# Scatter products of an expert: one two-bank PSUM tile and 1024-column adds

## The chip, the cores and the metric

The kernel runs on one core of a Trainium2 chip. The metric is the device time of one launch in microseconds (us). The time before is 1429.59 us, the median of three runs (1428.54 to 1430.69).

## The reference

One decoder block for 256 tokens of width 2048, all in float32: a mixing half (attention heads and a gated recurrence) and then a mixture of experts. Each token takes one of four groups of experts and two of the four experts in it. What matters here is the second half:

```python
for gi in range(N_GROUPS):
    sl = slice(gi * EXPERTS_PER_GROUP, (gi + 1) * EXPERTS_PER_GROUP)
    a = jnp.einsum('nd,edf->nef', hf, w_gate[sl])
    u = jnp.einsum('nd,edf->nef', hf, w_up[sl])
    hid = jax.nn.silu(a) * u * combine[:, sl, None]
    out = out + jnp.einsum('nef,efd->nd', hid, w_down[sl])
```

There are 16 experts of 2048 x 1024 (gate, up) and 1024 x 2048 (down), 24 MB each. `combine` is zero for the experts that a token does not take.

## The kernel before

The mixing half fills the first third of the time and ends at about 480 us. The change is in the expert loop behind it, from L845 on.

**One expert.** Its tokens, at most 64 (`CAP`), are collected by `gather(e)`, L763: eight matmuls with a 0/1 matrix, four into each of two PSUM tiles of 512 columns, one copy by ScalarE out of each tile (L777), then transposes (L783) and VectorE products (L786) into `xg`. The stages `ga` and `up` (L823) and `pd` (L880) each read eight pieces of weights of 1 MB. Two matmuls for the two halves of PSUM's partitions use 64 columns of the array each. ScalarE copies `pd` into `osb` (L883): 128 partitions, of which rows 0 to 63 hold the even blocks of 512 output columns and rows 64 to 127 the odd ones, for the same 64 tokens.

**Scatter.** `scatter(e)`, L805, brings these rows back to the tokens. For each half j of the columns, each half n of the tokens and each partition half z there is one matmul with 64 rows (L811) into a PSUM tile `psc` of 512 columns, and one add by VectorE (L813) into the accumulator `acc`: eight matmuls and eight adds. The scatter of an expert is written in the loop of the next one. That of expert 0 runs after `up` of expert 1, that of expert 1 between the pieces of `up` of expert 2, and those of experts 2 to 14 between the pieces of `ga` of the next expert. The last expert is different: its weights come in four blocks of columns (L893), each followed by four smaller scatter matmuls (L901) and adds (L906).

**PSUM.** `pscr()` gives tiles of one bank from two tags of two buffers each: `psc` for the products of gather and scatter, `pt` for transposes. With `ga`, `up` (one bank each) and `pd` (two) all eight banks are taken.

**Order.** The instructions of an engine are put in their order when the kernel is built, by a planner with costs of its own: where the next instruction by program order is not ready in its reckoning, it takes the next one that is. A tile of a tag is given out in program order, when the one before in its buffer has been read for the last time. So scatter and gather matmuls stand between the pieces of weights. On the chip each engine then works strictly in that order.

**Weights.** SyncE issues a load of 1 MB for each piece, over 19 slots in SBUF that are used in turn. A load waits until its slot has been read, and for the load eight before it.

Of the kernel before, what the change touches and what calls it, by code (L numbers as in the profile page):

```python
# [9 lines left out]
F32 = mybir.dt.float32  # L10
# [4 lines left out]
AF = mybir.ActivationFunctionType  # L15
ALU = mybir.AluOpType
# [3 lines left out]
P = 128  # L20
# [17 lines left out]
def hybrid_block_kernel(  # L38
# [8 lines left out]
    mm = nc.tensor.matmul  # L47
    V = nc.vector
    S = nc.scalar
# [8 lines left out]
    def area(s, shape, dtype=F32, name="ar"):  # L58

        return arena.tile(shape, dtype, name=name, tag=f"a{s}")  # L60
# [161 lines left out]
    def slot_of(idx):  # L222
        return first[idx] if idx < NSLOT else cycle[(idx - NSLOT) % len(cycle)]
# [158 lines left out]
    for col, w in half1:  # L382
        j, c = w // P, col // P
# [233 lines left out]
    x2 = X  # L617
# [133 lines left out]
    pq = tc.alloc_tile_pool(name="pq", bufs=1, space=PSUM)  # L751
# [5 lines left out]
    def piece(e, kind, i):  # L757
        return loaded.pop((e * 3 + kind) * 8 + i)

    def pscr(tag="psc"):  # L760
        return pq.tile([P, 512], F32, name=tag, tag=tag, bufs=2)

    def gather(e):  # L763

        pg = mp.tile([P, NT, CAP], F32, name="pg")
        for n in range(NT):
            V.tensor_scalar(pg[:, n], slot[:, :CAP], rk[:, n, e:e + 1], r2[:, n:n + 1],  # L767
                            ALU.is_equal, ALU.mult)
        xn = mp.tile([P, 2, 512], F32, name="xn")
        for j in range(2):  # L770
            ps = pscr()
            for n in range(NT):
                for z in range(2):
                    b = 2 * j + z
                    mm(ps[64 * z:64 * z + 64], pg[:, n], x2[:, n, b * 512:(b + 1) * 512],  # L775
                       start=n == 0, stop=n == 1)
            S.activation(xn[:, j], ps, AF.Copy)  # L777
        xg = mp.tile([P, NC, CAP], F32, name="xg")
        for j in range(2):
            pt = pscr("pt").rearrange("p (q z s) -> p q z s", q=4, z=2)  # L780
            xq = xn[:, j].rearrange("s (p q) -> s q p", q=4)
            for q in range(4):
                nc.tensor.transpose(pt[:, q].rearrange("p z s -> p (z s)"), xq[:, q], ident)  # L783
            for z in range(2):
                c0 = (2 * j + z) * 4
                V.tensor_tensor(xg[:, c0:c0 + 4], pt[:, :, z],  # L786
                                gfe[:, c0:c0 + 4].unsqueeze(2).to_broadcast([P, 4, CAP]),
                                ALU.mult)
        return xg

    def scatter_matrix(e):
        pcm = mp.tile([P, NT, P], F32, name="pcm")
        for n in range(NT):
            V.tensor_scalar(pcm[:, n], slot, rk[:, n, e:e + 1], comb[:, e // 4, n, e % 4:e % 4 + 1],
                            ALU.is_equal, ALU.mult)
        pt = pscr("pt").rearrange("p (n s) -> p n s", n=4)
        for n in range(NT):
            nc.tensor.transpose(pt[:, n], pcm[:, n], ident)
        pT = mp.tile([P, NT, P], F32, name="pT")
        V.tensor_copy(pT, pt[:, 0:2])  # L800
        return pT

    acc = [None, None]

    def scatter(e, pT, osb):  # L805
        for j in range(2):
            for n in range(NT):
                for z in range(2):
                    lo = 64 * z
                    ps = pscr()  # L810
                    mm(ps, pT[lo:lo + 64, n], osb[lo:lo + 64, j], start=True, stop=True)  # L811
                    bs = slice((2 * j + z) * 512, (2 * j + z + 1) * 512)
                    V.tensor_tensor(acc[n][:, bs], x2[:, n, bs] if e == 0 else acc[n][:, bs],  # L813
                                    ps, ALU.add)

    def stream(ps, xg, e, kind):
        for i in range(8):
# [11 lines left out]
    def final_gain():  # L829
        sl = [slot_of((NE - 1) * 24 + i) for i in (5, 6, 7)]  # L830
        gf = area(sl[0], [P, D], name="gf")
        y = [area(sl[1 + n], [P, D], name=f"y{n}") for n in range(NT)]
        for q in range(4):
            ps = pscr("pt").rearrange("p (c f) -> p c f", c=4)
            for c in range(4):
                mm(ps[:, c], ident[0:16, 4 * q + c:4 * q + c + 1].to_broadcast([16, P]), frow,
                   start=True, stop=True)
            S.activation(gf[:, q * 512:(q + 1) * 512], ps.rearrange("p c f -> p (c f)"), AF.Copy)
        return sl, gf, y
# [5 lines left out]
    for e in range(NE):  # L845
        ga = pq.tile([P, 512], F32, name="ga")
        up = pq.tile([P, 512], F32, name="up")
        stream(ga, xg, e, 0)
        if e == NE - 1:
            sl, gf, y = final_gain()  # L850
        stream(up, xg, e, 1)
        if e == 0:
            for n in range(NT):
                acc[n] = area(alias[n], [P, D], name=f"acc{n}")
            work = area(alias[2], [P, 2048], name="work")
            osb = work[:, 0:1024].rearrange("p (j f) -> p j f", j=2)
            hid = work[:, 1024:1536]
            hT = work[:, 1536:2048].rearrange("p (j s) -> p j s", j=4)
        silu = S.activation(hid, ga, AF.Silu).ins
        if e == NE - 1:  # L860
            with tc.issue_after(silu):
                S.activation(rf[:, 0:1], rf[:, 0:1], AF.Sqrt)
        V.tensor_tensor(hid, hid, up, ALU.mult)  # L863
        if pend is not None:
            scatter(*pend)
        pT = scatter_matrix(e)
        if e + 1 < NE:
            xg = gather(e + 1)
        pt = pscr("pt").rearrange("p (j s) -> p j s", j=4)
        for j in range(4):  # L870
            nc.tensor.transpose(pt[:, j], hid[:, j * P:(j + 1) * P], ident)
        V.tensor_copy(hT, pt)  # L872
        pd = pq.tile([P, 2, 512], F32, name="pd")
        if e < NE - 1:
            for i in range(8):
                wt = piece(e, 2, i)
                z, j = i // 4, i % 4
                for blk in range(4):
                    lo = 64 * (blk % 2)
                    mm(pd[lo:lo + 64, blk // 2], hT[:, j, z * 64:z * 64 + 64],  # L880
                       wt[:, blk * 512:(blk + 1) * 512], start=i == 0, stop=i == 7)
                advance()
            S.activation(osb, pd, AF.Copy)  # L883
            pend = (e, pT, osb)
# [3 lines left out]
    for b in range(4):  # L888
        for hf in range(2):
            wt = piece(NE - 1, 2, 2 * b + hf).rearrange("p (c f) -> p c f", c=4)  # L890
            for j in range(4):
                for z in range(2):
                    mm(pd[64 * z:64 * z + 64, b % 2, 0:256], hT[:, j, hf * 64:hf * 64 + 64],  # L893
                       wt[:, j, z * 256:(z + 1) * 256], start=hf == 0 and j == 0,
                       stop=hf == 1 and j == 3)
        S.activation(osl[:, b], pd[:, b % 2, 0:256], AF.Copy)
        bs = slice(b * 512, (b + 1) * 512)
        pz = [pscr() for z in range(2)]
        for n in range(NT):
            for z in range(2):  # L900
                mm(pz[z][:, n * 256:(n + 1) * 256], pT[64 * z:64 * z + 64, n],  # L901
                   osl[64 * z:64 * z + 64, b], start=True, stop=True)
        for n in range(NT):
            for z in range(2):
                zs = slice(b * 512 + z * 256, b * 512 + z * 256 + 256)
                V.tensor_tensor(acc[n][:, zs], acc[n][:, zs], pz[z][:, n * 256:(n + 1) * 256],  # L906
                                ALU.add)
        for n in range(NT):
            jk = cst.tile([P, 512], BF16, name="jk", tag="jk", bufs=1)
            S.activation(jk, acc[n][:, bs], AF.Square, accum_out=fs[:, n, b:b + 1])  # L910
            (V if b == 3 else nc.gpsimd).tensor_tensor(y[n][:, bs], acc[n][:, bs], gf[:, bs],
                                                       ALU.mult)
# [14 lines left out]
    with tc.If(nover > CAP):  # L927
        with tc.tile_pool(name="ovp", bufs=1, space=PSUM) as ovp:
# [3 lines left out]
            for n in range(NT):  # L932
                xs = area(free.pop(), [P, D], name="xs")
                V.tensor_scalar(xs, x2[:, n], r2[:, n:n + 1], None, ALU.mult)
                for c in range(NC):
                    pt = ovp.tile([P, P], F32, name="pt", tag="pt", bufs=2)
# [7 lines left out]
            with tc.For_i(0, NE, 1) as e:  # L944
# [12 lines left out]
                for fb in range(2):  # L957
                    for kind, src in ((0, w_gate), (1, w_up)):
                        ps = ovp.tile([P, NT, 512], F32, name="ps", tag="ps", bufs=2)
# [10 lines left out]
                    for j in range(4):  # L970
                        for n in range(NT):
                            pt = ovp.tile([P, P], F32, name="pt", tag="pt", bufs=2)
                            nc.tensor.transpose(pt, hd[:, n, j * P:(j + 1) * P], ident)
                            V.tensor_copy(hTo[:, 4 * fb + j, n * P:(n + 1) * P], pt)
                for b in range(4):
                    ps = ovp.tile([P, NT, 512], F32, name="ps", tag="ps", bufs=2)
                    for c in range(0, 8, 4):
                        wt = rows4(w_down, c, b * 512)
                        for k in range(4):
                            for n in range(NT):  # L980
                                mm(ps[:, n], hTo[:, c + k, n * P:(n + 1) * P], wt[:, k],
                                   start=c + k == 0, stop=c + k == 7)
                    for n in range(NT):
                        bs = slice(b * 512, (b + 1) * 512)
# [38 lines left out]
```

## Time and profile before

| | |
|---|---|
| median of 3 runs | 1429.59 us |
| the profiled execution | 1428.93 us |
| its span, first to last instruction | 1427.2 us |
| busy share: PE, VectorE (DVE), ScalarE (ACT), GpSimd | 95%, 31%, 19%, 1% |
| mean granted clock of TensorE | 0.996 |
| moved by DMA | 483.79 MB |

Times in the profile are counted from the first instruction. PE is TensorE's matmuls, PEld its weight loads, SPq the queue of SyncE. A float32 matmul stands as two records, so "x2" on L811, L775, L823 or L880 is one matmul of the program, and a piece of weights is "x8". In the rows, "x4" after a time counts instructions that were merged because nothing else of that engine came between, and the brackets hold the idle time before them and what ended it.

### The profile page before, as it was taken

Reading aid. Unit: us, or ns where it says so; the run is one execution under the profiler, and the core shown is the slowest. Engines: PE = TensorE matmul, PEld = TensorE weight load, DVE = VectorE, ACT = ScalarE, POOL = GpSimd, SP = SyncE. Lnnn points to the kernel's source line nnn. Section 1 sums busy time; section 2 is a strip of 40 time slices with the busy share of each in tenths; the row PEclk is TensorE's granted clock in tenths of the full one; section 3 lists DMA queues with packets and bytes.
Section 4 is the critical chain, followed back from the end, with each engine's and each line's share of the span. In section 5 each row is a group of like instructions: output and inputs, shape, how many; then the busy total and the mean of one; then the engine's idle time right before and its main releaser. Section 6 shows DMA issues by size and latency. Waiting matters only on the chain.

```text
span 1427.2 us, 16870 instructions
## 1 busy us (share of the span) xinstructions
PE 1357.8 (95%) x7073; PEld 737.6 (52%) x7073; DVE 439.8 (31%) x714; ACT 273.7 (19%) x408; POOL 18.0 (1%) x47
## 2 busy tenths in 40 slices
PE   7999999999999999999999999999999999999995
PEld 6999898898887633433332332323323333233333
DVE  4554557557555410221112111111111111211012
ACT  5453543533533300000000000000000000000012
POOL 2000000000000000000000000000000000000002
PEclk9999999999999999999999999999999999999998
DMA  6566553555697699999999999999999999999995
GB/s 229 186 210 169 162 176 120 176 177 178 219 343 292 228 384 418 422 421 422 420 421 422 421 422 421 422 420 421 421 422 422 420 422 421 421 421 421 421 413 214
DMA packets 111648, 483.79 MB, mean 339 GB/s; under 512 B 19728, under 2 KB 21968, under 8 KB 63440
## 3 DMA queue, kind: packets, MB, share of 16 engines
q1 hardware_dynamic: 110912, 482.62, 85.5%
q8 instruction: 57, 0.93, 0.3%
q14 instruction: 23, 0.19, 0.0%
q10 hardware_dynamic: 656, 0.04, 0.0%
HBM read 480.54 MB, written 2.10 MB: 338 GB/s over the span
## 4 chain that ended last, share of the span: by engine, by line
PE 94%; DVE 2%; ACT 1%; issue 1%; DMA 0%; SPq 0%; DVEq 0%; ACTq 0%
PE ga L823 16%; PE up L823 16%; PE pd L880 15%; PE psc L811 7%; PE pp L310 5%; PE pp L312 5%; PE pp L311 5%; PE pp L293 4%; PE pp L295 4%; PE pp L296 4%; PE psc L775 4%; PE pt L783 1%; PE pw L414 1%; PE pd L893 1%; ACT work L883 1%
## 5 line engine op out<-in xcount | busy, mean ns | idle before, releaser
L823 PE MATMUL ga<-wt,xg 128*64 128x512 f32 x1024 | 272.3, 601 | 0.0
L823 PE MATMUL up<-wt,xg 128*64 128x512 f32 x1024 | 228.0, 595 | 0.0
L263 DVE TENSOR_TENSOR whl<-raw,whl 128x1024 fp32r<-128x1024 f32 x144 | 175.6, 1224 | 136.1 <-ACT whl L262 135.9
L880 PE MATMUL pd<-wt,work 128*64 128x512 f32 x960 | 210.0, 594 | 4.0 <-DVE work L872 4.0
L262 ACT ACTIVATE whl<-raw 128x1024 fp32r<-128x1024 f32 x144 | 152.0, 1058 | 233.4 <-PE pp L312 121.5
L813 DVE TENSOR_TENSOR acc<-acc,psc 128x512 f32<-128x512 f32 x112 | 74.4, 686 | 378.3 <-PE psc L811 378.3
L823 PEld LDWEIGHTS ga<-wt,xg 128*64 128x64 f32 x1024 | 78.8, 136 | 149.0 <-issue 139.8
L293 PE MATMUL pp<-hTh,whl 128*128 128x256 f32 x512 | 147.7, 288 | 3.1 <-ACT hTh L328 3.1
L295 PE MATMUL pp<-hTl,whl 128*128 128x256 f32 x512 | 146.5, 286 | 0.9 <-DVE hTl L329 0.9
L296 PE MATMUL pp<-hTh,whl 128*128 128x256 f32 x512 | 146.2, 286 | 0.0
L823 PEld LDWEIGHTS up<-wt,xg 128*64 128x64 f32 x1024 | 72.5, 137 | 135.0 <-issue 127.7
L880 PEld LDWEIGHTS pd<-wt,work 128*64 128x64 f32 x960 | 69.2, 137 | 134.3 <-issue 123.9
L811 PE MATMUL psc<-work,pT 64*128 64x512 f32 x240 | 99.7, 642 | 16.5 <-ACT work L883 15.4
L293 PEld LDWEIGHTS pp<-hTh,whl 128*128 128x128 f32 x512 | 99.4, 194 | 4.2 <-ACT hTh L328 4.0
L295 PEld LDWEIGHTS pp<-hTl,whl 128*128 128x128 f32 x512 | 99.4, 194 | 1.5 <-DVE hTl L329 1.4
L296 PEld LDWEIGHTS pp<-hTh,whl 128*128 128x128 f32 x512 | 99.4, 194 | 0.0
L883 ACT ACTIVATE work<-pd 128x1024 f32<-128x1024 f32 x15 | 15.3, 1023 | 429.0 <-PE pd L880 429.0
L775 PE MATMUL psc<-X,pg 128*64 128x512 f32 x256 | 94.8, 596 | 0.7 <-DVE pg L767 0.7
L863 DVE TENSOR_TENSOR work<-work,up 128x512 f32<-128x512 f32 x16 | 11.0, 687 | 244.4 <-PE up L823 244.4
L777 ACT ACTIVATE xn<-psc 128x512 f32<-128x512 f32 x32 | 19.0, 595 | 308.2 <-PE psc L775 308.2
L310 PE MATMUL pp<-whl,hTh 128*128 128x512 f32 x192 | 77.6, 404 | 0.0
L312 PE MATMUL pp<-whl,hTl 128*128 128x512 f32 x192 | 75.4, 393 | 0.0
(240 smaller groups left out, 1054.7 us busy)
## 6 DMA issues: line engine op xcount, KB each, us to landing
wt<-in_w_gate_dram SPq DMA_DIRECT2D x128, 1024.0 KB, 19.8
wt<-in_w_up_dram SPq DMA_DIRECT2D x128, 1024.0 KB, 19.8
wt<-in_w_down_dram SPq DMA_DIRECT2D x126, 1024.0 KB, 19.8
raw<-in_w_in_dram SPq DMA_DIRECT2D x55, 1024.0 KB, 5.2
raw<-in_w_out_dram SPq DMA_DIRECT2D x16, 1024.0 KB, 5.3
X<-in_x_dram SPq DMA_DIRECT2D x4, 512.0 KB, 7.1
wt<-in_w_down_dram SPq DMA_DIRECT2D x4, 512.0 KB, 11.4
out_dram<-y SPq DMA_DIRECT2D x4, 512.0 KB, 4.3
```

Source lines behind the costliest of these rows:

```text
L262: S.activation(t[:, 0], raw[:, k * hf:k * hf + k], AF.Copy)
L263: V.tensor_tensor(t[:, 1], raw[:, k * hf:k * hf + k], t[:, 0].bitcast(F32), ALU.subtract)
L293: mm(o, hi[:, k, cs], ah, start=st and j % 2 == 0, stop=False, skip_group_check=True)
L295: mm(o, hi[:, k, cs], al, start=False, stop=False, skip_group_check=True)
L296: mm(o, lo[:, k, cs], ah, start=False, stop=sp, skip_group_check=True)
L310: mm(pp[:, n], ah, hi[:, k], start=c == c0, stop=False)
L312: mm(pp[:, n], al, hi[:, k], start=False, stop=c == c1 - 1)
L775: mm(ps[64 * z:64 * z + 64], pg[:, n], x2[:, n, b * 512:(b + 1) * 512], start=n == 0, stop=n == 1)
L811: mm(ps, pT[lo:lo + 64, n], osb[lo:lo + 64, j], start=True, stop=True)
L813: V.tensor_tensor(acc[n][:, bs], x2[:, n, bs] if e == 0 else acc[n][:, bs], ps, ALU.add)
L823: mm(ps[64 * z:64 * z + 64], xg[:, c], wt[:, o:o + 512], start=c == 0, stop=c == NC - 1)
L880: mm(pd[lo:lo + 64, blk // 2], hT[:, j, z * 64:z * 64 + 64], wt[:, blk * 512:(blk + 1) * 512], start=i == 0, stop=i == 7)
```

## The change

`psc` becomes a tile of two banks with one buffer, where there were two buffers of one bank. In `gather` both halves j go into one tile. In `scatter` the products of z = 0 and z = 1 go into the two banks of one tile, and one add over 1024 columns takes the place of two over 512. The last expert's blocks take their two product tiles as the two banks of one. The bytes of PSUM are the same, and so are the matmuls.

```diff
-    def pscr(tag="psc"):
-        return pq.tile([P, 512], F32, name=tag, tag=tag, bufs=2)
+    def pscr():
+        return pq.tile([P, 512], F32, name="pt", tag="pt", bufs=2)
+
+    def ptwo():
+
+        return pq.tile([P, 2, 512], F32, name="psc", tag="psc", bufs=1)
...
         xn = mp.tile([P, 2, 512], F32, name="xn")
+        ps = ptwo()
         for j in range(2):
-            ps = pscr()
...
-                    mm(ps[64 * z:64 * z + 64], pg[:, n], x2[:, n, b * 512:(b + 1) * 512],
+                    mm(ps[64 * z:64 * z + 64, j], pg[:, n], x2[:, n, b * 512:(b + 1) * 512],
                        start=n == 0, stop=n == 1)
-            S.activation(xn[:, j], ps, AF.Copy)
+            S.activation(xn[:, j], ps[:, j], AF.Copy)
...
     def scatter(e, pT, osb):
         for j in range(2):
             for n in range(NT):
+                ps = ptwo()
                 for z in range(2):
                     lo = 64 * z
-                    ps = pscr()
-                    mm(ps, pT[lo:lo + 64, n], osb[lo:lo + 64, j], start=True, stop=True)
-                    bs = slice((2 * j + z) * 512, (2 * j + z + 1) * 512)
-                    V.tensor_tensor(acc[n][:, bs], x2[:, n, bs] if e == 0 else acc[n][:, bs],
-                                    ps, ALU.add)
+                    mm(ps[:, z], pT[lo:lo + 64, n], osb[lo:lo + 64, j], start=True, stop=True)
+                bs = slice(j * 1024, (j + 1) * 1024)
+                V.tensor_tensor(acc[n][:, bs], x2[:, n, bs] if e == 0 else acc[n][:, bs],
+                                ps.rearrange("p z f -> p (z f)"), ALU.add)
...
-        pz = [pscr() for z in range(2)]
+        p2 = ptwo()
+        pz = [p2[:, z] for z in range(2)]
```

## Rows read from the trace of the kernel before

**Rows 1.** A stretch of the run, PE to POOL: busy us by engine, granted clock, DMA share, GB/s.
```profile
540.00:1380.00 840.00, 798.36 (x3476) 273.62 (x3473) 137.11 (x273) 43.48 (x64) 0.00 (x0) 1.00 1.01 421
```
**Rows 2.** Waits of PE from 540 us: total us, times, longest; the two largest.
```profile
PE pt L871 <- DVE xg L786: 19.7, 14, 1.6
PE psc L811 <- ACT work L883: 15.4, 13, 1.2
```
**Rows 3.** The chain that ended last: start us, us, work; two experts' down stages.
```profile
1044.99 13.98 PE pd L880 x64
...
1103.07 13.98 PE pd L880 x64
```
**Rows 4.** Timeline of SyncE's queue: start us, us; loads of eight pieces each.
```profile
1070.63 17.74 SPq L236 DMA_DIRECT2D wt<-in_w_down_dram  x8
1090.51 17.73 SPq L233 DMA_DIRECT2D wt<-in_w_gate_dram  x8
```
**Rows 5.** Timeline of PE at the end: the last block of the last expert.
```profile
1408.49 3.67 PE L893 MATMUL pd<-wt,work 128*64 128x256 f32 x32
```
**Rows 6.** Line L242, last ten loads: durations ns, first and last start; landing.
```profile
L242 SPq DMA_DIRECT2D wt<-in_w_down_dram x10: 368/1242/9264, 1370.3 to 1397.7; - x10
...
DMA to landing us min/median/max: 11.3/14.0/20.7
```
**Rows 7.** Timeline of PE: scatter of expert 9 between the pieces of `ga`.
```profile
1060.12 1.12 PE L811 MATMUL psc<-work,pT 64*128 64x512 f32 x2 [1.18 <-ACT work L883]
1061.18 1.94 PE L823 MATMUL ga<-wt,xg 128*64 128x512 f32 x8
1063.04 1.12 PE L811 MATMUL psc<-work,pT 64*128 64x512 f32 x2
...
1065.96 1.13 PE L811 MATMUL psc<-work,pT 64*128 64x512 f32 x4
...
1074.74 1.12 PE L811 MATMUL psc<-work,pT 64*128 64x512 f32 x2
1075.79 0.64 PE L775 MATMUL psc<-X,pg 128*64 128x512 f32 x1
```
**Rows 8.** Groups of VectorE by shape, whole run: busy us, mean ns, idle before.
```profile
L813 DVE TENSOR_TENSOR acc<-acc,psc 128x512 f32<-128x512 f32 x112 | 74.4, 686 | 378.3 <-PE psc L811 378.3
...
L567 DVE TENSOR_TENSOR kq<-pp,rd 128x1024 f32<-128x1024 f32 x2 | 2.5, 1226 | 0.6 <-PE pp L296 0.6
```
**Rows 9.** Timeline of all engines: the scatter of expert 0.
```profile
570.07 1.13 PE L811 MATMUL psc<-work,pT 64*128 64x512 f32 x4
...
571.23 1.28 DVE L813 TENSOR_TENSOR acc<-X,psc 128x512 f32<-128x512 f32 x2 [0.29 <-PE psc L811]
571.97 1.72 PE L811 MATMUL psc<-work,pT 64*128 64x512 f32 x4 [0.77 <-DVE acc L813]
...
577.80 3.65 PE L775 MATMUL psc<-X,pg 128*64 128x512 f32 x16
```
**Rows 10.** Timeline of PE: the scatter of expert 1 and the gather behind it.
```profile
617.26 1.13 PE L811 MATMUL psc<-work,pT 64*128 64x512 f32 x4
...
620.18 1.12 PE L811 MATMUL psc<-work,pT 64*128 64x512 f32 x2
...
628.96 1.12 PE L811 MATMUL psc<-work,pT 64*128 64x512 f32 x2
...
631.78 3.60 PE L775 MATMUL psc<-X,pg 128*64 128x512 f32 x16
```
**Rows 11.** Timeline of all engines: the first gather, and a matmul of the second.
```profile
491.87 0.60 ACT L777 ACTIVATE xn<-psc 128x512 f32<-128x512 f32 x1 [1.07 <-PE psc L775]
...
492.44 1.07 PE L775 MATMUL psc<-X,pg 128*64 128x512 f32 x2
...
493.45 0.75 PE L783 MATMUL pt<-ident,xn 128*128 128x128 f32 x4
```
**Rows 12.** Line L233, loads issued from 585 to 592 us.
```profile
DMA to landing us min/median/max: 10.9/11.7/12.5
```

More of the change, by code (lines that the diff above doesn't have):

```diff
@@ L774, in gather @@
                     b = 2 * j + z
-                    mm(ps[64 * z:64 * z + 64], pg[:, n], x2[:, n, b * 512:(b + 1) * 512],
+                    mm(ps[64 * z:64 * z + 64, j], pg[:, n], x2[:, n, b * 512:(b + 1) * 512],
                        start=n == 0, stop=n == 1)
-            S.activation(xn[:, j], ps, AF.Copy)
+            S.activation(xn[:, j], ps[:, j], AF.Copy)
         xg = mp.tile([P, NC, CAP], F32, name="xg")
         for j in range(2):
-            pt = pscr("pt").rearrange("p (q z s) -> p q z s", q=4, z=2)
+            pt = pscr().rearrange("p (q z s) -> p q z s", q=4, z=2)
             xq = xn[:, j].rearrange("s (p q) -> s q p", q=4)
@@ L795, in scatter_matrix @@
                             ALU.is_equal, ALU.mult)
-        pt = pscr("pt").rearrange("p (n s) -> p n s", n=4)
+        pt = pscr().rearrange("p (n s) -> p n s", n=4)
         for n in range(NT):
@@ L833, in final_gain @@
         for q in range(4):
-            ps = pscr("pt").rearrange("p (c f) -> p c f", c=4)
+            ps = pscr().rearrange("p (c f) -> p c f", c=4)
             for c in range(4):
@@ L868, in hybrid_block_kernel @@
             xg = gather(e + 1)
-        pt = pscr("pt").rearrange("p (j s) -> p j s", j=4)
+        pt = pscr().rearrange("p (j s) -> p j s", j=4)
         for j in range(4):
```

## The prediction

> **What bounds the kernel now.** I read the stretches first, then PE's waits, the chain, SyncE's queue and the end of the run. From 540 to 1380 us two things are full at once: the DMA engines (share 1.01, 421 GB/s) and PE (798.36 of 840 us, granted clock 1.00); VectorE is busy 137 us of 840 [rows 1]. Which one sets the end? PE's two largest waits there are for other engines, 19.7 and 15.4 us over the experts, and no wait for a load is of that size [rows 2]. So PE is the chain. It needs 1103.07 - 1044.99 = 58.08 us for an expert [rows 3]. The loads take 1090.51 - 1070.63 = 19.88 us for eight pieces, 59.64 us for the 24 of an expert [rows 4]. PE thus eats up its lead in loaded weights by 1.6 us with each expert, and at the end little of it is left: the last load is issued at 1397.7 and takes at least 11.3 us, so it lands at 1409.0 or later [rows 6], and the half block that reads it starts at 1408.49 + 3.67 / 2 = 1410.3 [rows 5]. That is the key to the case: time added to PE's chain comes out at the end in full, while of time taken from it about 1.3 us can be cashed before the loads are the bound. With the last load's two halves used apart it is 3.67 / 4 = 0.9 us more, 2.2 at most.
>
> **The change part by part.** *Adds.* Eight of 0.686 us become four over 1024 columns. A 1024-column product with an input of two PSUM banks stands in the trace at 1.226 us [rows 8]; bounds are 1.22 and 2 x 0.686 = 1.37. An expert's adds fall from 5.49 to 4.90 us, on an engine that waits 378 us for these very products [rows 8]: nothing on the path.
>
> *Matmuls in the steady experts.* The number of matmuls is the same. What counts is how they stand: one alone occupies PE for 1.12 us and two neighbours (z = 0 and 1) together for 1.13 us [rows 7], so the halves run side by side when adjacent. In the 13 `ga` stages from expert 3 on, the eight stand before the pieces as 1, 1, 2, 2, 1, 1 (the two groups left out in [rows 7] are a pair and a single): six groups, and a group costs PE 1061.18 - 1060.12 = 1.06 us. Four groups would be the least. Will the new tile draw the halves together? I think not by itself. The single at the start had two free buffers and still stood alone, so it was not the buffer that parted the halves but the length of the gap that the planner saw before the next piece. The new tile changes nothing in the lengths of gaps. The places 1, 1, 2, 2, 1, 1 happen to fall on whole tiles (first, second; pair; pair; seventh, eighth), so that no tile has to wait within a gap. I take 0 per expert; one group more or fewer would be +-1.06 us, 13.8 us over 13 experts.
>
> *The wait that one buffer adds.* The first matmul of a tile now waits for the last one's add. By [rows 9] an add starts 571.23 - 570.07 = 1.16 us after its pair; it lasts 1.23, and PE resumes 0.05 us after an add's end (571.23 + 0.69 = 571.92, 571.97): 2.44 us from pair to pair. Queued behind the waiting matmul on PE is everything, the pieces of weights first. Between two tiles in a `ga` stage stands a piece, 1063.04 - 1061.18 = 1.86 us, and the next pair comes 1.06 + 1.86 = 2.92 us after the last [rows 7]: hidden, with 0.48 us to spare. Without the piece a tile stalls PE for 2.44 - 1.06 = 1.38 us. The gather matmul that now follows the eighth product at once (1074.74, then 1075.79 [rows 7]) can't be given its tile there any more; I expect it one piece later, at no cost.
>
> The Trainium skill ("Trainium Kernel Development and Optimization", Best Practices) says to double-buffer for performance, which speaks against this change; by it each of the four tiles in 13 experts would show its stall, and the estimate is the second rival below under its worst condition. The rows above say that the piece between covers it.
>
> *Expert 0's scatter* has no pieces between. Now the gather behind it starts at 577.80, 7.73 us after the first pair [rows 9]. Four tiles of 2.44 us and then the gather, which needs the same buffer: 9.76 us, **+2.0 us**.
>
> *Expert 1's scatter* stands as 2, 1, 2, 2, 1 in five gaps of `up` (the two pairs in the middle are left out in [rows 10]), with the gather right behind the stage at 631.78. These places do not fall on whole tiles: 2 | 1 | 1 (the next tile is not free) | 2 | 1, and the eighth product is left for after the stage, where the gather has to wait 2.44 us for it: +2.4. If the first gap comes a piece later, four groups and one tile behind, 4 x 1.06 + 2.44 against 5 x 1.06: +1.4. If places happen to fit, 0; if two tiles are left, +3.8. I take **+2.0 us**, between the nearest two.
>
> *First gather.* One matmul of the second gather now stands between two transposes at 492.44, while ScalarE's copy ends at 491.87 + 0.60 = 492.47 and the transposes go on at 493.45 [rows 11]. With one buffer it can't stand there, as the first gather's tile is free only after that copy; the transposes go at 492.55: **-0.9 us**. It joins its seven fellows later, where the halves run in twos: nothing.
>
> *Loads.* SyncE's queue issues when a slot is read, so PE's 2 us come to the loads too. Where the lead is thinnest, after expert 0's scatter, loads land 10.9 us or more after they are issued [rows 12]: work is queued for 2 us of delay and more. Nothing. *Last expert.* Before the next block's products PE has a whole block of L893 to do, 3.67 us [rows 5]; the four adds of 256 columns that free the tile take less than four of 512, 2.74 us [rows 8]: nothing, and the halves stay in two banks as they were.
>
> Sum: -0.9 + 2.0 + 2.0 + 0 = **+3.1 us**. Against the profiled execution that is 1428.93 + 3.1 = 1432.0; the median of the three runs lies 0.66 us above it, so I give **1432.7**. Own range: -0.9 to +5.8, 1428.7 to 1435.4.
>
> **Rivals.** (1) *The halves do come together*, four or five groups in each steady expert: PE saves 13.8 to 27.6 us, more than the 4 us above, and then waits for weights. The loads end as now, up to 0.9 us earlier because the first slots are read earlier, and 1.3 to 2.2 us are left to win: 1426.5 to 1428.3, say 1427.8. For it: the matmuls of a tile now stand next to each other in the program. Against it: so did they before.
> In a sentence of its own: the Trainium skill, "TensorEngine Tiling (Array Packing)", Key Properties, says that tiles of the array run in parallel and that a change of the tiling mode drains TensorE; [rows 7] agree with both (a pair costs what a single costs, 1.13 and 1.12 us).
> (2) *Slower by much*: the planner's gaps shift against the tiles, so that one group more is formed in each steady expert, +13.8 us, 1446.5 with the +3.1; or a tile follows a tile without a piece between, 1.38 us each time, 13 x 1.38 = 18 us for one such place (four: 72 us, 1504). It decides from the point where the piece between is missing or the add takes over 1.7 us. For it: scatter 1's places show that gaps and tiles don't fit by themselves. Against it: the spare 0.48 us.
> (3) *The change moves nothing*: other ready work fills the two early stalls, 1428.5 to 1430.
>
> **How the numbers follow.** Forecast 0.60, rival 1 0.18, rival 2 0.15, rival 3 0.07. About 0.2%, 2.9 us, is what can be told from no change here: slower begins at 1432.45. The forecast lies on that line, so I split it, 0.30 slower and 0.30 same. Rival 1 gives 0.13 same and 0.05 faster, rival 2 0.15 slower, rival 3 0.06 same and 0.01 faster: faster 0.06, same 0.49, slower 0.45. The range 1427.0 to 1442.0 leaves out most of rival 2 and the best end of rival 1, some 0.18.
>
> **What would show it.** In the profile after: L813 x60 near 1.23 us; the gather behind expert 0's scatter about 9.8 us after the first pair; L811 still in six groups in the late `ga` stages; PE waits "psc L811 <- DVE acc L813" of some 1.4 us three times and no more; the transposes at 492.5; the DMA share still 1.01, and the last piece landing near 1409. Wrong would be: four groups with PE waiting for `wt` loads (rival 1), seven or more groups or many waits for L813 (rival 2), or an add well over 1.37 us.

## The result, and the profile after

The changed kernel takes 1463.71 us (median of 4 runs, 1462.98 to 1465.34) against 1429.32 us for the kernel before, run beside it: a ratio of 1.0241, 95% interval 1.0223 to 1.0259. That is 34.4 us slower; the forecast was 3.1 us slower, and the time lies outside the range. In the code after, the gather's matmuls are line 779, its copies 781, its transposes 787, the scatter's matmuls 815, the adds 817, the streams `ga` and `up` 827, `pd` 884 and its eviction 887.

The page first: the clock of TensorE in 40 slices, and the group of the wide adds (count, busy us, mean ns, idle before).

```profile
PEclk9999999999999999989999999999999999999998
...
L817 DVE TENSOR_TENSOR acc<-acc,psc 128x1024 f32<-128x1024 f32 x56 | 68.4, 1221 | 372.2 <-PE psc L815 372.2
```

The adds came out as sized (1.221 us against the 1.226 of [rows 8]). New is an 8 in the middle of the clock line. The same stretch as [rows 1], and three short ones (columns: PE, PEld, DVE, ACT, POOL busy, granted clock, DMA share, GB/s):

```profile
540.00:1380.00 840.00, 783.07 (x3330) 257.74 (x3328) 125.33 (x208) 39.43 (x56) 0.00 (x0) 0.98 1.01 418
577.00:584.00 7.00, 5.07 (x12) 1.11 (x12) 2.12 (x3) 0.00 (x0) 0.00 (x0) 0.56 1.02 422
639.00:652.00 13.00, 9.85 (x22) 2.52 (x23) 2.93 (x5) 0.96 (x2) 0.00 (x0) 0.51 1.01 420
949.90:953.30 3.40, 3.38 (x8) 1.01 (x10) 0.47 (x2) 0.00 (x0) 0.00 (x0) 0.50 1.01 422
```

PE is busy for 15 us less than before and does 146 records less. The clock fell to its lower level of 1.2 GHz (0.50) at 577.8 us for 6.8 us, at 639.3 for 13.7, and six times later for 3.4 us, each time at the start of a `pd` stage; before, it stood at 1.00 here. PE's waits from 540 us, the answer to [rows 2]:

```profile
PE pt L875 <- DVE xg L790: 19.7, 13, 1.6
PE psc L815 <- ACT work L887: 14.2, 12, 1.2
PE psc L779 <- ACT xn L781: 9.8, 13, 0.8
PE psc L815 <- DVE acc L817: 7.2, 6, 1.3
PE pd L884 <- DVE work L876: 4.1, 12, 0.3
PE psc L779 <- DVE acc L817: 2.6, 2, 1.3
```

The first two and the fifth are old. The third is new and was nowhere in the prediction: a gather matmul waits for ScalarE's copy. The fourth and sixth are the wait for an add that the prediction priced.

The time by stages, from one start of `pd` to the next in PE's timeline (us). Columns 3 and 4 are two of the experiments below:

| from `pd` of expert | before | after | 11: late copies | 7: late copies, two buffers |
|---|---|---|---|---|
| 0 to 1 | 54.87 | 61.27 | 61.08 | 52.97 |
| 1 to 2 | 53.92 | 63.91 | 57.89 | 54.74 |
| 2 to 3 | 58.08 | 57.10 | 56.46 | 57.7 |
| later, no clock fall | 58.08 | 59.03 | 57.74 | 57.74 |
| later, with one | none | 60.7 | 59.3 | 59.3 |
| falls from `pd` 3 on | 0 | 6 | 2 | 2 |

The two profiled spans are 1463.6 and 1427.2 us, 36.4 apart. Of these 6.4 + 10.0 - 1.0 us came in the first three rows, and 20.5 in the twelve steady periods: 0.95 us in each, and 1.7 us more in those with a fall (12 x 0.95 + 6 x 1.7 = 21.6, of which the last two periods give back about 1). Expert 0's scatter in PE's timeline after (start, us, work, in brackets the idle time before and who ended it), beside [rows 9]:

```profile
570.26 1.13 PE L815 MATMUL psc<-work,pT 64*128 64x512 f32 x4
...
572.71 1.13 PE L815 MATMUL psc<-work,pT 64*128 64x512 f32 x4 [0.96 <-DVE acc L817]
575.16 1.13 PE L815 MATMUL psc<-work,pT 64*128 64x512 f32 x4 [1.32 <-DVE acc L817]
577.62 1.91 PE L815 MATMUL psc<-work,pT 64*128 64x512 f32 x4 [1.32 <-DVE acc L817]
580.84 3.68 PE L779 MATMUL psc<-X,pg 128*64 128x512 f32 x8 [1.31 <-DVE acc L817]
585.27 1.94 PE L779 MATMUL psc<-X,pg 128*64 128x512 f32 x8 [0.76 <-ACT xn L781]
```

Pairs start 2.45 and 2.46 us apart (2.44 forecast), until the clock falls: the fourth pair takes 1.91 us in place of 1.13, the first half of the gather 3.68 in place of the 1.94 of the second. And expert 1's, beside [rows 10]:

```profile
629.81 1.12 PE L815 MATMUL psc<-work,pT 64*128 64x512 f32 x2
...
632.73 1.12 PE L815 MATMUL psc<-work,pT 64*128 64x512 f32 x2
...
635.16 1.13 PE L815 MATMUL psc<-work,pT 64*128 64x512 f32 x4 [0.94 <-DVE acc L817]
637.62 1.13 PE L815 MATMUL psc<-work,pT 64*128 64x512 f32 x4 [1.32 <-DVE acc L817]
640.07 2.08 PE L815 MATMUL psc<-work,pT 64*128 64x512 f32 x4 [1.32 <-DVE acc L817]
643.47 3.68 PE L779 MATMUL psc<-X,pg 128*64 128x512 f32 x8 [1.32 <-DVE acc L817]
647.91 3.68 PE L779 MATMUL psc<-X,pg 128*64 128x512 f32 x8 [0.76 <-ACT xn L781]
```

Only the first tile stands between pieces of `up`; three tiles and the gather were left behind the stage, one after another. The steady experts, first and last group of the scatter, the start of the gather behind the next piece, and the start of its second half:

```profile
1086.48 1.12 PE L815 MATMUL psc<-work,pT 64*128 64x512 f32 x2 [1.18 <-ACT work L887]
...
1089.40 1.12 PE L815 MATMUL psc<-work,pT 64*128 64x512 f32 x2
...
1101.09 1.12 PE L815 MATMUL psc<-work,pT 64*128 64x512 f32 x2
1102.14 1.94 PE L827 MATMUL ga<-wt,xg 128*64 128x512 f32 x8
1103.91 1.45 PE L779 MATMUL psc<-X,pg 128*64 128x512 f32 x5
...
1106.97 0.59 PE L779 MATMUL psc<-X,pg 128*64 128x512 f32 x1
1108.31 0.64 PE L779 MATMUL psc<-X,pg 128*64 128x512 f32 x1 [0.75 <-ACT xn L781]
```

The scatter stands as before: six groups 2.92 us apart, no wait for an add. The new wait is in the gather, 13 times from 540 us.

### The profile page after: what moved, and what is told of

The parts are those of the page before. It is cut to its first block, busy times and chain, and to the rows that moved or that the text cites. A ratio compares the mean times of both kernels' runs of the same rounds, so it can differ in the third digit from the quotient of the medians.

```text
span 1463.6 us, 16838 instructions
## 1 busy us (share of the span) xinstructions
PE 1375.3 (94%) x7073; PEld 731.6 (50%) x7073; DVE 433.0 (30%) x654; ACT 275.0 (19%) x408; POOL 17.9 (1%) x47
## 4 chain that ended last, share of the span: by engine, by line
PE 93%; DVE 3%; ACT 2%; DMA 1%; issue 1%; SPq 0%; ACTq 0%; DVEq 0%
PE ga L827 15%; PE up L827 15%; PE pd L884 15%; PE psc L815 6%; PE pp L310 5%; PE pp L312 5%; PE pp L311 5%; PE psc L779 5%; PE pp L293 4%; PE pp L295 4%; PE pp L296 4%; PE pt L787 2%; PE pw L414 1%; PE pd L897 1%; ACT work L887 1%
## 5 line engine op out<-in xcount | busy, mean ns | idle before, releaser
L827 PE MATMUL ga<-wt,xg 128*64 128x512 f32 x1024 | 262.8, 602 | 0.0
L827 PE MATMUL up<-wt,xg 128*64 128x512 f32 x1024 | 238.5, 594 | 0.0
L884 PE MATMUL pd<-wt,work 128*64 128x512 f32 x960 | 219.3, 616 | 4.1 <-DVE work L876 4.1
L817 DVE TENSOR_TENSOR acc<-acc,psc 128x1024 f32<-128x1024 f32 x56 | 68.4, 1221 | 372.2 <-PE psc L815 372.2
L827 PEld LDWEIGHTS ga<-wt,xg 128*64 128x64 f32 x1024 | 71.4, 136 | 155.8 <-issue 154.9
L827 PEld LDWEIGHTS up<-wt,xg 128*64 128x64 f32 x1024 | 75.5, 137 | 139.2 <-issue 136.2
L779 PE MATMUL psc<-X,pg 128*64 128x512 f32 x256 | 101.5, 641 | 14.6 <-ACT xn L781 11.2
L887 ACT ACTIVATE work<-pd 128x1024 f32<-128x1024 f32 x15 | 15.4, 1024 | 415.4 <-PE pd L884 415.4
```

Of the source, the lines that this page charges most:

```text
L779: mm(ps[64 * z:64 * z + 64, j], pg[:, n], x2[:, n, b * 512:(b + 1) * 512], start=n == 0, stop=n == 1)
L827: mm(ps[64 * z:64 * z + 64], xg[:, c], wt[:, o:o + 512], start=c == 0, stop=c == NC - 1)
L884: mm(pd[lo:lo + 64, blk // 2], hT[:, j, z * 64:z * 64 + 64], wt[:, blk * 512:(blk + 1) * 512], start=i == 0, stop=i == 7)
```

## The experiments

The ratios are to the kernel before on the same chip. "Falls" are stretches at the 1.2 GHz level after the first three experts unless a time is given; that at the very end, which every kernel has, is not counted. Falls and stage times are those of the one profiled execution of each kernel. The number of falls differs between executions of one kernel (the last section has the kernel before), so a fall more or less decides nothing by itself.

**1. One copy for both halves** of the gather's tile, in the changed kernel:

```diff
-            S.activation(xn[:, j], ps[:, j], AF.Copy)     # in the loop over j
+        S.activation(xn, ps, AF.Copy)                     # after it
```

> The changed kernel with one difference: the gather's tile is copied out by one 1024-column copy after all eight matmuls, so that no matmul of the gather has to wait for a copy of the same tile. Theory A (that wait, 0.76 us in each gather, and the fall of the granted clock that follows it cost the steady experts their 1.6 us; the one buffer costs only the two early scatters): the steady experts go back from 59.6 to about 58.1 us each, the clock falls only near the two early scatters, and some 14 us of the early loss stay: 1443 us (1438 to 1448). Theory B (the steady loss comes from the scatter, its wide add or its one buffer): 1458 us or more, and the steady experts stay at 59 us or more.

Measured: 1442.56 us, ratio 1.0089 (1.0072 to 1.0105). The wait of line 779 for ScalarE is gone, the steady period is 57.74 us, and three falls are left, one of them at `pd` 3, the first that counts. In the main as Theory A had it: 21 of the 34 us hang on how the tile is copied out. (This run changes two things, the place of the copies and their number; 6 and 11 change the place alone.)

**2. The change of the gather alone,** on the kernel before, in the banks of `pd`:

```diff
+        ps = pq.tile([P, 2, 512], F32, name="pd", tag="pd")
         for j in range(2):
-            ps = pscr()
...
-                    mm(ps[64 * z:64 * z + 64], pg[:, n], ...
+                    mm(ps[64 * z:64 * z + 64, j], pg[:, n], ...
...
-            S.activation(xn[:, j], ps, AF.Copy)
+            S.activation(xn[:, j], ps[:, j], AF.Copy)
```

> The kernel before with only the gather's part of the change: both halves of its products in one two-bank tile (lent by the banks of pd, which are free then), copied half by half; the scatter is as before, with two buffers of one bank and adds of 512 columns. Theory A: the wait of 0.76 us appears in each of the 16 gathers, some 11 us, with some falls of the clock on top, no early loss: 1443 us (1437 to 1449). Theory B: no more than the spread from before, 1428 to 1432 us.

Measured: 1456.96 us, ratio 1.0204 (1.0180 to 1.0229), well above the range of Theory A, and far from B. The wait is there, and steady periods are 59.1 us, or 60.8 with a fall; there are six falls. So the gather's new tile makes most of the loss without any change in the scatter, and the clock's part, for which the expectation had left two or three us, is about 10 us of it (six falls at 1.7 us).

**3. The changed kernel with two buffers** for the new tile, `pd` sharing them:

```diff
-        return pq.tile([P, 2, 512], F32, name="psc", tag="psc", bufs=1)
+        return pq.tile([P, 2, 512], F32, name="psc", tag="psc", bufs=2)
...
-        pd = pq.tile([P, 2, 512], F32, name="pd")
+        pd = pq.tile([P, 2, 512], F32, name="pd", tag="psc", bufs=2)
```

> The changed kernel with two buffers of the two-bank tile instead of one; the second takes the place of pd's banks, which come from the same buffers. Theory A: the early loss (15 us) is gone, the gather's wait for the copy stays: about 1446 us (1440 to 1450), with a steady expert still at 59 us or more. Theory B (the one buffer is behind all of it): 1428 to 1432 us.

Measured: 1455.15 us, ratio 1.0179 (1.0162 to 1.0196). The early stages are back at 53.95 and 55.55 us, the steady loss stays. The time lies 5 us above the range; one fall more than in the changed kernel (1.7 us) and a third stage of 59.10 us in place of 57.10 are the larger part of that.

**4. Waits of the first two scatters filled** with useless matmuls, the rest as changed:

```diff
+                if e < 2:
+                    fill = pscr()
+                    for i in range(9):
+                        mm(fill[:, 0:P], pT[:, n], ident, start=True, stop=True)
```

> The changed kernel, with nine 128-column matmuls of no use between the tiles of the first two scatters, where PE stands still for 1.3 us each time. They don't shorten the wait for the add. Theory A (PE's standing still lets the granted clock fall, and the matmuls behind then run at half speed for 6.8 and 13.7 us, which costs about 10 us of the early loss): the clock stays at 1.00 from 560 to 660 us, and the time falls by 8 to 10 us to 1454 us (1451 to 1457). If the waits themselves are the early loss: 1463 us or a little more, since the filling takes PE's time.

Measured: 1464.17 us, ratio 1.0241. A miss: nine matmuls take 2.27 us, more than the wait, so tiles came every 3.27 us. The clock stays at 1.00 from 575 to 655 us, though, and nearly all that this gives back goes into the longer cycle; a seventh fall takes the rest.

**5. The same with four matmuls,** pinned behind the pair that the wait follows:

```diff
+                if e < 2 and (j, n) != (1, 1):
+                    with tc.issue_after(last.ins):
+                        fill = pscr()
+                        for i in range(4):
+                            mm(fill[:, 0:P], ident, ident, start=True, stop=True)
```

> The changed kernel with four 128-column matmuls of no use behind each of the first three tiles of the first two scatters. In the run with nine of them they took 2.27 us, more than the wait of 1.3 us, and a tile came every 3.27 us instead of 2.45; four take some 1.0 us and fit the wait. Theory A (standing still lets the clock fall, and the fall has its own price): the clock stays at 1.00 around 575 to 655 us, a tile still comes every 2.45 us, and the time is about 1457 us (1453 to 1460). If the fall of the clock costs nothing there, 1463 us.

Measured: 1459.10 us, ratio 1.0205 (1.0190 to 1.0221). The stretch of the two early scatters, of this kernel and then of the changed one:

```profile
575.00:655.00 80.00, 74.54 (x348) 27.80 (x348) 16.69 (x30) 4.01 (x6) 0.00 (x0) 1.00 1.01 421
```
```profile
575.00:655.00 80.00, 70.08 (x277) 22.51 (x277) 14.74 (x27) 4.01 (x6) 0.00 (x0) 0.87 1.00 412
```

With the waits filled, the clock holds, and the stages take 58.76 and 59.10 us in place of 61.27 and 63.91: 7.3 us of the early loss is the clock, lost because PE stood still between the tiles. (A seventh fall later takes part of it back.)

**6. Experiment 2 with both copies after the eight matmuls** in the program:

```diff
+        for j in range(2):
             S.activation(xn[:, j], ps[:, j], AF.Copy)     # a loop of its own
```

> The run with the gather's part alone, with one difference: both copies of the gather's tile stand in the program behind its eight matmuls, as two copies of 512 columns. Theory A' (the wait of 0.76 us is no property of the two banks or of the copies: it is there because the second half's matmuls stand in the program behind a read of the same tile): no PE wait for the copy in the gathers but for that of the transposes, a steady expert at 57.7 to 58.1 us, 1428 to 1431 us. If two banks of one tile disturb each other whatever the order: 1450 us or more.

Measured: 1432.29 us, ratio 1.0015 (0.9998 to 1.0032), a little over what was expected. No wait for ScalarE at the gather's matmuls; steady period 57.74 us, three falls. The same tile, copies and matmuls as in 2: 24.7 us hang on the order of these lines alone.

**7. Two buffers and late copies,** 3 and 6 together with the scatter as changed:

> Both causes taken away: two buffers of the two-bank tile (shared with pd), and the gather's two copies behind its eight matmuls. The wide adds stay. Theory A': the early loss and the gather's wait are both gone, the adds cost nothing: as before, or up to 2 us less where PE saves time and the loads become the bound: 1426.5 to 1430 us. If the wide add or the two-bank tile has a cost of its own: 1433 us or more.

Measured: 1429.33 us, ratio 0.9998 (0.9989 to 1.0007). The wide tile and the wide add in themselves cost nothing and bring nothing that lasts: 0.34 us an expert are won (57.74 against 58.08), two falls (1.6 us each) and the last two stages take most of it.

**8. The gather's wait filled** with three useless matmuls, on the kernel of 3:

```diff
+            if j == 0:
+                with tc.issue_after(last.ins):
+                    fill = pscr()
+                    for i in range(3):
+                        mm(fill[:, 0:P], ident, ident, start=True, stop=True)
```

> The run with two buffers and the gather's wait (1455 us), with three 128-column matmuls of no use in the wait of 0.76 us between the gather's halves, some 0.7 us; the wait stays as long. Theory A (the falls of the granted clock in the steady experts, seven of 3.4 us, follow from PE standing still in each gather): the falls go or become few, each steady expert takes 59.1 to 59.4 us, and the time is 1443 to 1447 us. If the falls come from elsewhere they stay, and the time is 1455 us or a little more.

Measured: 1456.37 us, ratio 1.0189. The wait has gone from the list of PE's waits, seven falls stay. A miss, and a useful one: what lets the clock fall in the steady experts is not that PE stands still in the gather.

**9. The pause ahead of `pd`,** on the kernel of 3. Eight useless matmuls were to run while PE waits for `hid`:

```diff
+        with tc.issue_after(last):                        # last matmul of up
+            fill = pscr()
+            for i in range(8):
+                mm(fill[:, 0:P], ident, ident, start=True, stop=True)
```

> The kernel with two two-bank buffers took 1455.2 us, with seven falls of the granted clock of 3.4 us each in the steady experts, every one at the start of a pd stage; each costs about 1.7 us. Here eight useless 128-column matmuls (about 1.26 us) are pinned behind the last matmul of up, where PE otherwise stands still for 1.6 us before the transposes of hid. Theory A (this pause ahead of pd is what lets the clock fall): no fall in the steady experts, period 59.1 us throughout, 1443 us (1441 to 1445). Rival B (the falls are decided elsewhere): still six or seven falls, 1454 to 1457 us.

Measured: 1468.50 us, ratio 1.0272 (1.0255 to 1.0289), with no fall from 540 us to 1454 us. PE's timeline, and the stretch of the steady experts:

```profile
1126.67 2.02 PE L877 MATMUL pt<-ident 128*128 128x128 f32 x16 [1.62 <-DVE xg L790]
1128.53 0.60 PE L880 MATMUL pt<-ident,work 128*128 128x128 f32 x4
...
1129.91 13.95 PE L889 MATMUL pd<-wt,work 128*64 128x512 f32 x64 [0.56 <-DVE work L881]
```
```profile
660.00:1400.00 740.00, 691.94 (x3092) 244.06 (x3090) 109.11 (x178) 33.68 (x48) 0.00 (x0) 1.00 1.01 418
```

The filling landed behind the pause, not in it: the 1.62 us are still there, and 1.84 us were added (period 60.94 in place of 59.10). So the experiment did not do what it was made for, and the time is a miss. Still, with the pause kept at its length and the gather's wait kept too, the clock never fell.

**10. The kernel before, made longer:** the first four matmuls of `pd` twice, in experts 3 to 14, no wait added:

```diff
+                if i == 0 and e > 2:
+                    for blk in range(4):
+                        lo = 64 * (blk % 2)
+                        mm(pd[lo:lo + 64, blk // 2], hT[:, j, z * 64:z * 64 + 64],
+                           wt[:, blk * 512:(blk + 1) * 512], start=True, stop=True)
```

> The kernel before with the first four matmuls of pd issued twice in each expert from 3 to 14: 0.93 us more of full PE work in an expert, no wait added or moved, period 58.08 + 0.93 = 59.0 us, 12 experts. Theory A (the falls come from where the pause ahead of pd lies in time, which the expert's period shifts, and not from the gather's wait): falls of 3.4 us at some pd starts, three to seven of them at 1.7 us, 1429.4 + 11.2 + 5 to 12 = 1445 to 1453 us. Rival B (the gather's wait or the new tile is needed for a fall): no fall, 1440.6 us (1439 to 1442).

Measured: 1468.44 us, ratio 1.0275 (1.0251 to 1.0299). One `pd` start, and the window around it:

```profile
1122.84 0.63 PE L871 MATMUL pt<-ident,work 128*128 128x128 f32 x4 [1.62 <-DVE xg L786]
1123.51 0.41 PE L798 MATMUL pt<-ident,pcm 128*128 128x128 f32 x2
1124.26 3.57 PE L881 MATMUL pd<-wt,work 128*64 128x512 f32 x8 [0.34 <-DVE work L872]
```
```profile
1124.00:1128.00 4.00, 3.75 (x10) 1.14 (x12) 0.71 (x3) 0.00 (x0) 0.00 (x0) 0.57 1.01 422
```

Eleven falls, one in each of the twelve lengthened experts but the first. The expectation sized the four matmuls at 0.93 us; by [rows 3] an eighth of a `pd` stage is 13.98 / 8 = 1.75, and 12 x 1.75 + 11 x 1.6 = 38.6 us against the 38.4 measured. That is far above the range given, but the direction is Theory A's: neither the new tile nor its wait is needed for a fall. Work that never waits, added to the kernel before, brings one in nearly every expert. As the work stands at the start of `pd` itself, this run can't tell the longer period from the fuller `pd` start.

**11. The changed kernel, one buffer, late copies** (the edit of 6):

> The changed kernel, its one buffer kept, with the two copies of the gather put after its eight matmuls in the program. Theory A (the loss in the steady experts is the order of the second half's matmuls behind the first copy): the 0.76 us wait for ScalarE is gone, the steady period is 57.7 us, the early loss of 9 to 16 us stays: 1442 us (1439 to 1446), as with one copy. Rival B (one buffer costs the steady experts as well): above 1450 us.

Measured: 1437.21 us, ratio 1.0061 (1.0038 to 1.0085), 1.8 us below the range of Theory A. PE's waits, and expert 1's last tile and gather:

```profile
PE psc L816 <- DVE acc L818: 5.9, 5, 1.3
PE pd L885 <- DVE work L877: 4.1, 12, 0.3
PE psc L779 <- DVE acc L818: 2.6, 2, 1.3
PE pt L788 <- ACT xn L782: 2.3, 3, 0.8
```
```profile
637.67 1.13 PE L816 MATMUL psc<-work,pT 64*128 64x512 f32 x4 [1.32 <-DVE acc L818]
640.12 5.03 PE L779 MATMUL psc<-X,pg 128*64 128x512 f32 x16 [1.32 <-DVE acc L818]
```

Here two tiles, not one, found room in `up`, and the gather runs in one stretch.

**12. Two adds of 512 columns on the new tile:**

```diff
-                bs = slice(j * 1024, (j + 1) * 1024)
-                V.tensor_tensor(acc[n][:, bs], ..., ps.rearrange("p z f -> p (z f)"), ALU.add)
+                for z in range(2):
+                    bs = slice((2 * j + z) * 512, (2 * j + z + 1) * 512)
+                    V.tensor_tensor(acc[n][:, bs], ..., ps[:, z], ALU.add)
```

> The changed kernel with its two-bank tile, but the tile is added in two instructions of 512 columns, as before, in place of one of 1024. Theory A (the wide add by itself brings and costs next to nothing): a tile's adds last 2 x 0.69 = 1.37 us in place of 1.22, so the early tiles come every 2.6 us in place of 2.45, some 1 us more in all: 1463 to 1467 us. Rival B (the wide add is the loss): 1450 us or less.

Measured: 1465.86 us, ratio 1.0254 (1.0236 to 1.0271), in the range of Theory A. Until the clock falls the early tiles come 2.51 us apart, in place of 2.45. The wide add is not the loss. Whether it saves time as a whole is not shown: the interval overlaps with that of the changed kernel (1.0223 to 1.0259), and this run has seven falls in place of six.

## Why the prediction was wrong, step by step

**The sum of the loss.** From 7 to 11 to the changed kernel one thing changes at a time (in 7 `pd` shares the buffers): 1429.3 (two buffers, late copies), 1437.2 (one buffer), 1463.7 (copies in the loop). So the one buffer costs 7.9 us, and the place of the first copy 26.5 us; together they are the 34.4. The other way round, over 3 (two buffers, copies in the loop, 1455.2), it is 25.8 us for the copies and 8.6 for the buffer. By the intervals of the ratios each of these four is good to within some 4 us.

**The step that failed** is the gather's. The prediction followed the new tile through the scatter and put the gather at nothing: its first matmul was to come "one piece later, at no cost", and the one of the second gather "joins its seven fellows later, where the halves run in twos: nothing". The first matmul did come one piece later; what was not asked is what the tile does between the gather's own two halves. In the kernel before, the two halves had a tile each, and the second half's matmuls ran while ScalarE copied the first. Now both are banks of one tile; the program's first matmul into bank 1, written after the copy of bank 0, waits for that copy's end: 0.75 us, 13 times. That the two touch different banks does not help. What is shown (1, 2, 6, 11) is that the wait comes with the tile and goes when the copies stand after the matmuls; that it is kept by tile and not by bank is the plain reading of it. The diff had it: `ps = ptwo()` moved out of the loop over `j`, with the copy left inside it.

**Adds:** right (1.221 us, and off the path in the steady experts; 12 shows that the wide add is not the loss, not that it saves time). **Matmuls in the steady experts, 0:** right for the scatter, whose six groups and hidden add wait are as forecast; wrong for the expert, which takes 0.95 us more. The gather's wait is 0.75 of it; the other 0.2 was not traced, and with late copies the expert falls by more than the wait, from 59.03 to 57.74 us (11). **Expert 0's scatter, +2.0:** the mechanism and the 2.44 us were right, the size was not: +6.4. The gather came 10.58 us after the first pair, not 9.8, since the clock fell in between; its own wait and its half-clock matmuls are the rest. **Expert 1's scatter, +2.0, at most 3.8:** +10.0. The prediction took the places in `up` as given and let at most two tiles fall behind the stage; three did, with the gather, and there PE stood still so often that the clock was at 1.2 GHz for 13.7 us. Experiment 5 puts 7.3 us of both on the clock. That standing still could cost clock as well as its own length had no term in the sum. **First gather, -0.9:** the streams do start at 493.33 us in place of 494.13, -0.8; the second gather's wait of 0.76 takes it back before the first `pd` (529.8 against 529.6). **Loads, nothing:** right; the last is issued at 1403.3 us, 5.6 later than before, and is far from late as PE is 36 us behind there. So all of PE's time came out at the end, as the first part of the prediction said. **Last expert, nothing:** from the last `pd` start to the end 34.7 us against 34.4.

**The rivals.** The second, slower by much, had the nearest times, but not its mechanism: no group more, and no wait in a steady scatter; the tiles without a piece between them, its other half, came only in the experts where the forecast had put them. The first and the third did not occur. Of the signs named, "PE waits for adds three times and no more" was wrong (8 times, 9.8 us).

The sentence of the Trainium skill on double-buffering ("Trainium Kernel Development and Optimization", Best Practices) speaks of overlapping DMA with compute; the prediction carried it over to a PSUM tile and set it aside for the steady experts. A second buffer of this tile was worth 7.9 us here (11 against 7), all of it in the first two scatters. One reading was too strong: [rows 7], said to agree with two properties of the array, show that a pair runs side by side; a drain at a change of mode they neither show nor exclude.

## What to carry to other kernels

When two tiles become two banks of one, list every reader of the old tiles: a matmul into the second bank that follows a read of the first in the program may wait for it, and moving the read behind the matmuls takes that away (26.5 us here). Price a buffer taken away where tiles follow each other with nothing between (7.9 us here), not in the steady state that hides it; and where PE is the bound, count with each new standstill a possible fall of its clock. Before blaming a new wait for a slower clock, add work without a wait to the kernel before and see whether the clock falls there too.

## What the runs showed of the hardware

In the changed kernel PE is busy for 94% of the span, and its granted clock still fell to 1.2 GHz. In the early scatters PE had stood still for 0.96 and 1.32 us between pairs before it fell, and filling these gaps prevented it (4, 5). The Trainium skill has this under "TensorE: Matmul & The Clock Gate", in the section "A second HAM failure mode: psum-queue depth-cycling", from another kernel: frequent short standstills between groups of matmuls let the clock swing. These rows agree.

The steady falls are another matter. All lie at the start of `pd`, behind a pause of 1.62 + 0.34 us that the kernel before has in each expert as well, in the profiled execution without a fall:

```profile
1044.90:1048.30 3.40, 3.31 (x16) 1.20 (x18) 0.54 (x3) 0.00 (x0) 0.00 (x0) 1.00 1.01 422
```

Sixteen records run there in the 3.4 us in which the changed kernel, at 949.9 us, does eight: a fall costs 1.7 us. From `pd` 3 on there were none at a period of 58.08 us (before), two or three at 57.74 (1, 6, 7, 11), six or seven at 59.03 to 59.15, eleven in twelve experts with 1.75 us of work added at the start of `pd` (10), and none at 60.94 (9, where the small matmuls also ran between the pause and `pd`). So filling the gather's wait changes nothing (8), and the same pause goes with few falls at one length of an expert and with many at another.

The period does not settle it alone. Of the 18 executions of the kernel before that were run beside 5 to 8, fifteen took 1428.4 to 1430.1 us at a mean granted clock of 0.995 to 0.997, and three took 1434.3 to 1434.5 us at 0.992; no profile of these three was kept, but at 1.7 us a fall they had about three each, an estimate from the times. The kernel of 6, with three falls in its profile, went from 1429.7 to 1435.5 us, and that of 2 from 1454.6 to 1462.4. That it matters where in time the pauses fall is the plain reading, and it is not shown. Why one expert is spared and another not is left open; a kernel in which the pause itself is filled was not run, as the one made for it put its matmuls behind the pause. For this case it means that some 10 us of the 34 (6 x 1.7) are not the length of any wait; they came together with a changed period. With the 7.3 us of the early scatters the clock is about half of the loss.
